# Layer 0: decayed keys and values turned by VectorE in squares of 32 and placed by DMA instead of turned by TensorE; six small operations moved from VectorE to ScalarE

## The chip, the cores and the metric

The kernel runs on one core of one Trainium2 chip. That core has a TensorE (PE in the profile, its weight loads PEld), a VectorE (DVE), a ScalarE (ACT), a GpSimd (POOL), and a SyncE (SP) whose queue issues DMAs; 16 DMA engines move the data. The metric is device microseconds of one launch, the median over runs.

## The reference

One inference step of a trunk of two layers: layer 0 mixes tokens with RWKV-7, layer 1 with differential attention. 512 prompt tokens and 32 sample tokens go through both layers; what the change touches lies in layer 0. Its token mixer, cut to what matters:

```python
def step(S, inp):
    r_t, k_t, v_t, w_t, kk_t, a_t = inp
    sa = jnp.einsum('bhvk,bhk->bhv', S, -kk_t)
    S = (S * w_t[:, :, None, :] + sa[..., None] * (kk_t * a_t)[:, :, None, :]
         + v_t[..., None] * k_t[:, :, None, :])
    return S, jnp.einsum('bhvk,bhk->bhv', S, r_t)
S_T, y = lax.scan(step, S0.astype(f32), xs)
mean = jnp.mean(y, axis=-1, keepdims=True)
var = jnp.mean(jnp.square(y - mean), axis=-1, keepdims=True)
```

There are 24 heads of 64; the state S of a head is 64x64. The projections r, k, v, the decay and the gates come from one matrix product of the normalized input with `rw_in`, in float32.

## The kernel before

Two heads are one **pair**: 128 partitions hold the two heads' 64 channels, and there are 12 pairs. The 512 prompt tokens of a pair are cut into 8 chunks of 64, and the 32 sample tokens are a ninth with a state of their own (tile SS, loaded from `state_rwkv`; PE turns it into `ps_si`). Within a chunk the recurrence is solved as a small triangular system, and only the state passes from chunk to chunk.

Per pair there is a **preparation**, `rw_prep`, a generator whose steps are set off one at a time. It makes the decay sums (`cum`, `de`), the square-root factors (`rr`, turned by PE into `ps_rt`, then `r`; used by `ps_b`), the decayed queries `zr` and decayed keys `bk` (channels on partitions, 128 columns for each chunk), the products `at` (sent by DMA to `sc1`, brought back as `m` for POOL's inversion in `rw_invert`), and at its end `bt` and `sv`: keys and values with tokens on partitions, which the recurrence uses as matmul operands. Then comes the **chain**, `rw_chain`: per chunk three matmuls into `ps_c` with copies between them, ending in the next state SB (VectorE, `chunk`). The first chunk has no state before it, and its SB is `ps_c` times the decay `dl`. After that `rw_outputs` and `rw_finish` normalize (`yt`, `gs`) and gate the result.

PE's time between these steps is filled with the main projection: `ps_g` matmuls, three for each product since float32 is carried as two parts (`hh`, `hl` for activations, `whi`, `wlo` for weights). A weight tile is loaded on SP into one of five `raw` buffers when the block two before it begins; ScalarE makes `whi` from it and VectorE `wlo`.

What sets the order: every engine, SP's queue too, works in the order in which the program issues (class `Queue`, `tie`). Pairs 0 and 1 are prepared with `FILL0` and `FILL1`, which count the `ps_g` matmuls set after each step. From then on the table `PLAN` has 23 rows for each pair's chain; a row names the steps of other pairs' work set there (`prep` 2 is the preparation of the pair two ahead) with due times, by which the `ps_g` are put between. The preparation of a pair so begins three pairs ahead and ends in the first rows of the pair before it. The last pair's last steps of preparation run at the end of pair 9, with the loads of the memory attention (`cmt`, turned by PE into `ps_ck`) right behind. One of the pairs also loads four `lam` rows for layer 1.

In `rw_prep` the end is three groups of four PE transposes, one into `ps_v` and two into `ps_bt`, each copied by ScalarE to `sv` (four copies) or `bt` (two).

Of the kernel before, what the change touches and what calls it, by code (L numbers as in the profile page):

```python
# [9 lines left out]
F32 = mybir.dt.float32  # L10
# [36 lines left out]
LATER = 0.75  # L47
FULL = ("full", 0, 0, 0)
PLAN = [
    [[("val", 0, 0.95, 0), ("prep", 2, 0.1, 0)], [("prep", 2, 0, 0.42)]],  # L50
    [[("prep", 2, 0, 1.04)], [("prep", 1, 0.53, 0)]],
    [[], [("prep", 1, 0, 0), ("prep", 2, 0.56, 1.0)]],
    [[("prep", 2, 0, 0)], [("prep", 2, 0, 1.0)]],
    [[("smp", 0, 0.11, 0.28), ("prep", 1, 0.4, 0)], [("prep", 2, 0, 0.86)]],
    [[("out", -1, 0.11, 0)], [("prep", 2, 0, 0.84)]],
    [[("prep", 2, 0, 1.1), ("smp", 0, 0.21, 0.29)], [("prep", 2, 0, 0.86)]],
    [[("prep", 2, 1.1, 1.37)], [("smp", 0, 0.21, 0)]],
# [4 lines left out]
    [[("prep", 2, 0.36, 0.43), ("at", 1, 0, 0)], [("fin", -1, 0, 0.84)]],  # L62
    [[("prep", 2, 0.36, 0.43), ("fin", -1, 0, 0)], [("prep", 3, 0, 0)]],
    [[("prep", 2, 0.25, 0)], []],
    [[("fin", -1, 0, 0.98), ("smp", 0, 0.11, 0)], [("prep", 2, 0.4, 0), ("prep", 3, 0, 0.6)]],
    [[("prep", 3, 0.53, 0), ("mrg", 1, 0, 0.86)], []],
    [[("prep", 3, 0.11, 0.17), ("mrg", 1, 0.9, 0), ("rsq", 0, 0, 1.5)], []],
    [[("prep", 3, 0.33, 0), ("fin", -1, 0, 0.88)], []],
# [25 lines left out]
CU = 8 * 65 + 33  # L94
# [14 lines left out]
class Trunk:  # L109
# [529 lines left out]
    def split_roots(self):  # L639

        rr, r = self.rr, self.r20[:, :NS]
        self.ve.tensor_copy(rr[:, :NS], r)
        self.ve.tensor_tensor(rr[:, NS : 2 * NS], r, rr[:, :NS].bitcast(F32), ALU.subtract)

    def rw_prep(self, st, rkv):

        nc, p, pr = self.nc, self.rp, st["pr"]
# [16 lines left out]
        for i in range(5):  # L664
            o, c = (32 * i, 0) if i < 4 else (0, P - TS)
# [24 lines left out]
        ch = lambda t: t[:, : 8 * 65].rearrange("p (c w) -> p c w", w=65)  # L690
# [13 lines left out]
        rr = self.rr  # L704
# [3 lines left out]
        de = p.tile([P, CW], F32, tag="de", name="de", bufs=1)  # L708
# [7 lines left out]
        self.ae.copy(r4[:], pst[:, :P])  # L716
        yield
        st["dl"] = dl = self.rb.tile([P, 9], F32, tag="dl", name="dl", bufs=4)
        self.ve.tensor_copy(dl[:, :8], ch(de[:])[:, :, 64])
        self.ve.tensor_copy(dl[:, 8:9], de[:, CU - 1 : CU])  # L720

        st["zr"] = zr = self.zr[pr % 3]
        bk = self.bk
# [12 lines left out]
        r = rkv["r"]()  # L736
# [32 lines left out]
        for q in range(2):  # L769

            yield
            ps = [self.psm.tile([P, 4, 2, 64], F32, tag="m", name="ps_at") for _ in range(2)]
            for j in range(4):
                c, i, a = 4 * q + j, j // 2, j % 2
# [35 lines left out]
        for s in range(2):  # L810
            yield
            v = rkv["v"]()
# [8 lines left out]
        ps = self.psm.tile([P, 512], F32, tag="m", name="ps_bts")  # L821
# [2 lines left out]
        bt[2] = self.rb.tile([P, 1, P], F32, tag="bts", name="bts", bufs=2)  # L824
        self.ae.copy(bt[2][:, 0, :], ps[:, :P])
        self.ae.copy(sv[2][:TS, 0, :], ps[P - TS :, P : 2 * P])
        for q in range(2):
            yield
            if q:
                ps = self.psm.tile([P, 512], F32, tag="m", name="ps_v")  # L830
                for i in range(4):
                    self.te.transpose(ps[:, i * P : i * P + P], v[:, i * P : i * P + P], self.ident[:])
                pv = ps[:].rearrange("p (j c) -> p j c", j=4)
                for u in range(2):
                    if u:
                        yield
                    sv[u] = self.rb.tile([P, 4, P], F32, tag="sv", name="sv", bufs=4)
                    self.ae.copy(sv[u][:64, 0:4:2, :], pv[:64, 2 * u : 2 * u + 2])
                    self.ae.copy(sv[u][64:, 1:4:2, :], pv[64:, 2 * u : 2 * u + 2])
                yield  # L840
            ps = self.psm.tile([P, 512], F32, tag="m", name="ps_bt")
            for j in range(4):
                c = 4 * q + j
                self.te.transpose(ps[:, j * P : j * P + P], bk[:, c * P : c * P + P], self.ident[:])
            bt[q] = self.rb.tile([P, 4, P], F32, tag="bt", name="bt", bufs=4)
            self.ae.copy(bt[q][:], ps[:].rearrange("p (j c) -> p j c", j=4))

    def rw_invert(self, st):

# [104 lines left out]
    def chunk(self, st, c, S, Snew):  # L954

        nc, H, yt = self.nc, self.H, st["yt"]
        e, zs, ro, A, cv, cb = self.place(st, c)
        i = c // 2
        yield
        ps = self.psc.tile([P, 4, P], F32, tag="c", name="ps_c")  # L960
        rhs = self.avz[:, e, i, :]
        sd = None
        if c:
            self.te.matmul(ps[:, 0, :], st["zr"][:, c * P : c * P + P], S[:], start=True, stop=True)
            self.ve.tensor_tensor(rhs[zs], ps[zs, 0, :], rhs[zs], ALU.add)
            yield

        self.te.matmul(ps[:, 1, :], A[0].rearrange("p h t -> p (h t)"), rhs, start=True, stop=True)
        for h in range(2):
            self.ae.copy(cv[zs, H[h]], ps[H[h], 1, H[h]])  # L970
        if c:
            self.ae.copy(yt[ro, i, :], ps[ro, 0, :])
            sd = self.rb2.tile([P, P], F32, tag="sd", name="sd", bufs=RB)
            self.ae.activation(sd[:], S[:], AF.Copy, scale=st["dl"][:, c : c + 1])
        yield
        self.te.matmul(ps[:, 2, :], cb, cv, start=True, stop=True)
        for hc in H:
            d = st["dl"][hc, c : c + 1]
            if c == 0:
                self.ve.tensor_scalar(Snew[hc, hc], ps[hc, 2, hc], d, None, ALU.mult)  # L980
            else:
                self.ve.scalar_tensor_tensor(Snew[hc, hc], ps[hc, 2, hc], d, sd[hc, hc], ALU.mult, ALU.add)

# [10 lines left out]
    def rw_sample(self, st):  # L994

        nc, p, pr = self.nc, self.rb2, st["pr"]
        sl = self.SS[0]
        for h in range(2):
            self.se.dma_start(sl[64 * h : 64 * h + 64, 64 * h : 64 * h + 64], self.a["state_rwkv"][0, 0, 2 * pr + h])
        yield  # L1000
        ps = self.psm.tile([P, 4, P], F32, tag="m", name="ps_si")
        self.te.transpose(ps[:, 0, :], sl[:], self.ident[:])
        S = p.tile([P, P], F32, tag="ssi", name="ssi", bufs=1)
        self.ve.tensor_copy(S[:], ps[:, 0, :])
        yield from self.chunk(st, 8, S, sl)
        yield
        self.state_out(sl, self.o[8][0, 0, 2 * pr : 2 * pr + 2])
# [84 lines left out]
    def rw_finish(self, st):  # L1092

        yield
        nc, p, pr = self.nc, self.rk0, st["pr"]
        yt, bv = st["yt"], st["bv"]
        y = yt[:].rearrange("p i (h v) -> p (i h) v", h=2)
        s = p.tile([P, 10], F32, tag="gs", name="gs", bufs=1)
        self.ve.tensor_reduce(s[:], y, AX.X, ALU.add)
        self.ve.tensor_scalar(s[:], s[:], 1.0 / 64, None, ALU.mult)  # L1100
        sh = [P, 10, 64]
        yield
        self.ve.tensor_tensor(y, y, s[:].unsqueeze(2).to_broadcast(sh), ALU.subtract)
        yield
        sq = p.tile([P, 10, 64], F32, tag="gsq", name="gsq", bufs=1)
        self.ae.activation(sq[:], y, AF.Square)
        yield
        self.ve.tensor_reduce(s[:], sq[:], AX.X, ALU.add)
        self.ve.tensor_scalar(self.q20[:, NS:], s[:], 1.0 / 64, GN_EPS, ALU.mult, ALU.add)
        yield  # L1110
        self.ve.tensor_tensor(y, y, self.r20[:, NS:].unsqueeze(2).to_broadcast(sh), ALU.mult)
        yield
        for q, c0, n in ((0, 0, TP), (1, TP, TS)):
            ps = (self.psm if q else self.psx).tile([P, 512], F32, tag="m" if q else "x", name="ps_y")
            if q == 0:
                for i in range(4):
                    self.te.transpose(ps[:, i * P : i * P + P], yt[:, i, :], self.ident[:])
            else:
                self.te.transpose(ps[:, :P], yt[:, 4, :], self.ident[:])
            self.ve.scalar_tensor_tensor(bv[:, c0 : c0 + n], ps[:, :n], self.lnw[:, pr : pr + 1], bv[:, c0 : c0 + n],  # L1120
                                         ALU.mult, ALU.add)
        yield
        sg = st["gate"]()
        self.ve.scalar_tensor_tensor(sg[:], sg[:], 0.5, bv[:], ALU.mult, ALU.mult)
        self.put(pr, sg)
# [1182 lines left out]
```

## Time and profile before

| what | number |
| --- | --- |
| median of 3 runs | 1349.31 us (1349.03 to 1351.66) |
| the profiled execution | 1349.83 us |
| its span, first to last instruction | 1348.1 us |
| mean granted clock of TensorE | 0.997 |
| DMA | 150.47 MB, 370805 packets, 163177 of them under 512 B |
| q1 (all of SP's DMAs) | 42.0% of 16 engines' span |

Layer 0 takes the first half of the span; the pairs' chains run from about 130 to 660 us, one pair every 44 us or so. In a group's row stand: line, engine, operation, output and inputs, partitions x elements, count, then busy time, mean nanoseconds of one, and the idle time in front of it with what ended it. L106 is the one line by which nearly all instructions are issued, so they are told apart by tile names. In a timeline row stand start, duration, engine, operation and tiles, and in square brackets the idle time before. SPq is SP's queue, and its rows give the time of issuing, not of moving.

### The profile page before, as it was taken

How to read it: one execution, taken by the hardware profiler on the slowest of the kernel's cores; microseconds unless marked ns; L12 is line 12 of the kernel's file. 1: busy time of each engine (PE TensorE's matmuls, PEld its weight loads, DVE VectorE, ACT ScalarE, POOL GpSimd, SP SyncE). 2: the span in 40 equal slices, each digit the busy share in tenths (PEclk: the TensorE clock that was granted, in tenths of full speed). 3: DMA queues.
4: the chain of work that ended last, by engine and by line, in shares of the span. 5: the costliest groups of instructions: out<-in, count | busy, mean ns of one | idle time of the engine just before them, and what ended most of it. 6: DMA issues, size and time to landing. Idle time of an engine off the chain costs nothing. (4 is left out here: it accounts for less than half of the span.)

```text
span 1348.1 us, 31624 instructions
## 1 busy us (share of the span) xinstructions
PE 1319.8 (98%) x11662; PEld 1264.6 (94%) x11662; DVE 956.5 (71%) x2391; ACT 813.1 (60%) x2258; POOL 368.0 (27%) x833
## 2 busy tenths in 40 slices
PE   8999999999999999999999999999999999999997
PEld 6988899999999998988999999999999999999997
DVE  5766878888887888675764578876588748887343
ACT  5766777877787777665543366754476546664222
POOL 2128668666776677600000000000000001002000
PEclk9999999999999999999999999999999999999999
DMA  7443322333233322342465466652367424762321
GB/s 225 145 138 76 82 57 68 85 87 92 59 96 87 75 78 70 100 124 83 115 188 138 130 192 149 145 141 79 98 154 160 110 83 108 164 148 89 94 86 68
DMA packets 370805, 150.47 MB, mean 112 GB/s; under 512 B 163177, under 2 KB 361202, under 8 KB 370650
## 3 DMA queue, kind: packets, MB, share of 16 engines
q1 hardware_dynamic: 370586, 148.43, 42.0%
q8 instruction: 92, 1.51, 0.5%
q14 instruction: 63, 0.52, 0.1%
q10 hardware_dynamic: 64, 0.02, 0.0%
HBM read 118.00 MB, written 30.18 MB: 110 GB/s over the span
## 5 line engine op out<-in xcount | busy, mean ns | idle before, releaser
L106 PE MATMUL ps_g<-hh,wlo 128*128 128x272 f32 x1808 | 536.1, 297 | 1.1 <-DVE wlo L106 1.0
L106 PE MATMUL ps_g<-hh,whi 128*128 128x272 f32 x1808 | 533.9, 296 | 1.0 <-DVE ats L106 0.7
L106 PE MATMUL ps_g<-hl,whi 128*128 128x272 f32 x1808 | 532.7, 295 | 1.0 <-DVE hl L106 0.7
L106 PEld LDWEIGHTS ps_g<-hh,whi 128*128 128x128 f32 x1808 | 341.1, 189 | 5.9 <-DVE ats L106 0.9
L106 PEld LDWEIGHTS ps_g<-hl,whi 128*128 128x128 f32 x1808 | 340.9, 189 | 3.9 <-DVE hl L106 1.9
L106 PEld LDWEIGHTS ps_g<-hh,wlo 128*128 128x128 f32 x1808 | 340.5, 189 | 3.0 <-DVE wlo L106 1.8
L106 DVE TENSOR_TENSOR wlo<-raw,whi 128x512 fp32r<-128x512 f32 x314 | 214.4, 693 | 106.3 <-ACT whi L106 102.0
L106 ACT CAST whi<-raw 128x512 fp32r<-128x512 f32 x314 | 188.9, 619 | 116.7 <-PE ps_g L106 64.9
L868 POOL TENSOR_TENSOR tm<-u,m 102x84 f32<-102x84 f32 (+23 forms) x341 | 138.8, 407 | 117.6 <-DMA m<-sc 71.2
L870 POOL TENSOR_TENSOR u<-u,tm 102x84 f32<-102x84 f32 (+23 forms) x341 | 158.5, 465 | 26.7
L106 PE MATMUL ps_g<-hi,wlo 128*128 128x272 f32 x512 | 147.8, 289 | 1.1 <-DVE wlo L106 1.1
L106 PE MATMUL ps_g<-hi,whi 128*128 128x272 f32 x512 | 147.7, 288 | 0.0
L106 PE MATMUL ps_g<-lo,whi 128*128 128x272 f32 x512 | 147.4, 288 | 0.0
L1339 POOL TENSOR_TENSOR lo<-og,hi 128x544 fp32r<-128x544 f32 x8 | 13.2, 1651 | 378.1 <-ACT hi L106 377.6
L106 PEld LDWEIGHTS ps_g<-hi,wlo 128*128 128x128 f32 x512 | 96.4, 188 | 1.6 <-DVE wlo L106 1.5
L106 PEld LDWEIGHTS ps_g<-hi,whi 128*128 128x128 f32 x512 | 96.6, 189 | 0.0
L106 PEld LDWEIGHTS ps_g<-lo,whi 128*128 128x128 f32 x512 | 96.4, 188 | 0.0
L106 ACT ACTIVATE pt<-ps_s,snm 128x128 f32<-128x128 f32 (+3 forms) x96 | 50.3, 527 | 57.1 <-DVE snm L106 57.1
L106 DVE SCALAR_TENSOR_TENSOR SB<-ps_c,dl,sd 64x64 f32<-64x64 f32 x168 | 47.4, 282 | 26.6 <-PE ps_c L106 20.9
L106 ACT COPY sv<-ps_c 64x64 f32<-64x64 f32 x192 | 39.6, 206 | 33.1 <-PE ps_c L106 31.2
L1803 POOL MEMSET qs<- 128x128 f32 x2 | 0.3, 206 | 188.9 <-PE ps_g L106 188.9
L106 ACT ACTIVATE sg<-ps_g 128x272 f32<-128x272 f32 x64 | 25.1, 394 | 40.2 <-PE ps_g L106 36.2
(397 smaller groups left out, 2523.1 us busy)
## 6 DMA issues: line engine op xcount, KB each, us to landing
raw<-in_rw_in_dram SPq DMA_DIRECT2D x114, 256.0 KB
raw<-in_df_in_dram SPq DMA_DIRECT2D x112, 256.0 KB
raw<-in_w_out_dram SPq DMA_DIRECT2D x64, 256.0 KB
oscr<-sg SPq DMA_DIRECT2D x16, 272.0 KB
lo<-oscr SPq DMA_DIRECT2D x16, 272.0 KB
m<-sc SPq DMA_DIRECT2D x33, 128.0 KB
raw<-in_w_mem_v_dram SPq DMA_DIRECT2D x16, 256.0 KB
out_dram<-kt SPq DMA_DIRECT2D x48, 64.0 KB
```

Source lines behind the costliest of these rows:

```text
L106: return lambda *a, **k: self.trunk.tie(self, issue(*a, **k))
L868: nc.gpsimd.tensor_tensor(tm[:, :n, :wd], u3[:, :n, kx : kx + 1].to_broadcast(sh), m3[:, kx : kx + 1, kx + 1 :].to_broadcast(sh), ALU.mult)
L870: nc.gpsimd.tensor_tensor(u3[:, :n, kx + 1 :], u3[:, :n, kx + 1 :], tm[:, :n, :wd], ALU.add)
L1339: (self.nc.gpsimd if g % 2 and self.o1 else self.ve).tensor_tensor(lo[:], t, hi[:].bitcast(F32), ALU.subtract)
L1803: nc.gpsimd.memset(t[:], 0.0)
```

## The change

The two groups `ps_bt` and the group `ps_v` of each pair go from PE, and their copies from ScalarE. In their place VectorE turns a 128x512 tile in squares of 32x32 (STREAM_TRANSPOSE); four DMAs put the squares where they belong in a scratch tensor in DRAM (`tscr`, rows of 32 floats), and one DMA (`bt`) or four (`sv`) bring the turned tile back. That is 12 placements and 6 fetches for each pair on SP. The small transposes into `ps_bts`, for the sample tokens, stay on PE.

Besides, ScalarE takes the copy into `rr`, two into `dl`, the two SB of chunk 0 and the copy `ssi`; the scaling of `gs` by 1/64 is folded into the subtraction after it. `PLAN` rows 0, 1, 2, 4 and 15 are set anew.

```diff
--- before.py
+++ after.py
@@ -47,11 +47,11 @@
 LATER = 0.75
 FULL = ("full", 0, 0, 0)
 PLAN = [
-    [[("val", 0, 0.95, 0), ("prep", 2, 0.1, 0)], [("prep", 2, 0, 0.42)]],
-    [[("prep", 2, 0, 1.04)], [("prep", 1, 0.53, 0)]],
-    [[], [("prep", 1, 0, 0), ("prep", 2, 0.56, 1.0)]],
+    [[("val", 0, 0.95, 0), ("prep", 2, 0.1, 0)], [("prep", 2, 0, 0), ("prep", 1, 0, 0.71), ("prep", 1, 0, 0.71)]],
+    [[("prep", 2, 0, 1.04)], []],
+    [[], [("prep", 2, 0.56, 1.0)]],
     [[("prep", 2, 0, 0)], [("prep", 2, 0, 1.0)]],
-    [[("smp", 0, 0.11, 0.28), ("prep", 1, 0.4, 0)], [("prep", 2, 0, 0.86)]],
+    [[("smp", 0, 0.11, 0.28), ("prep", 1, 0, 0)], [("prep", 2, 0, 0.86)]],
     [[("out", -1, 0.11, 0)], [("prep", 2, 0, 0.84)]],
     [[("prep", 2, 0, 1.1), ("smp", 0, 0.21, 0.29)], [("prep", 2, 0, 0.86)]],
     [[("prep", 2, 1.1, 1.37)], [("smp", 0, 0.21, 0)]],
@@ -62,7 +62,7 @@
     [[("prep", 2, 0.36, 0.43), ("at", 1, 0, 0)], [("fin", -1, 0, 0.84)]],
     [[("prep", 2, 0.36, 0.43), ("fin", -1, 0, 0)], [("prep", 3, 0, 0)]],
     [[("prep", 2, 0.25, 0)], []],
-    [[("fin", -1, 0, 0.98), ("smp", 0, 0.11, 0)], [("prep", 2, 0.4, 0), ("prep", 3, 0, 0.6)]],
+    [[("fin", -1, 0, 0.98), ("smp", 0, 0.11, 0)], [("prep", 2, 0, 0.71), ("prep", 3, 0, 0.6)]],
     [[("prep", 3, 0.53, 0), ("mrg", 1, 0, 0.86)], []],
     [[("prep", 3, 0.11, 0.17), ("mrg", 1, 0.9, 0), ("rsq", 0, 0, 1.5)], []],
     [[("prep", 3, 0.33, 0), ("fin", -1, 0, 0.88)], []],
@@ -639,7 +639,7 @@
     def split_roots(self):
 
         rr, r = self.rr, self.r20[:, :NS]
-        self.ve.tensor_copy(rr[:, :NS], r)
+        self.ae.copy(rr[:, :NS], r)
         self.ve.tensor_tensor(rr[:, NS : 2 * NS], r, rr[:, :NS].bitcast(F32), ALU.subtract)
 
     def rw_prep(self, st, rkv):
@@ -716,8 +716,8 @@
         self.ae.copy(r4[:], pst[:, :P])
         yield
         st["dl"] = dl = self.rb.tile([P, 9], F32, tag="dl", name="dl", bufs=4)
-        self.ve.tensor_copy(dl[:, :8], ch(de[:])[:, :, 64])
-        self.ve.tensor_copy(dl[:, 8:9], de[:, CU - 1 : CU])
+        self.ae.copy(dl[:, :8], ch(de[:])[:, :, 64])
+        self.ae.copy(dl[:, 8:9], de[:, CU - 1 : CU])
 
         st["zr"] = zr = self.zr[pr % 3]
         bk = self.bk
@@ -824,26 +824,38 @@
         bt[2] = self.rb.tile([P, 1, P], F32, tag="bts", name="bts", bufs=2)
         self.ae.copy(bt[2][:, 0, :], ps[:, :P])
         self.ae.copy(sv[2][:TS, 0, :], ps[P - TS :, P : 2 * P])
+        scr = [self.dp.tile([TP, P], F32, tag=f"tscr{n}", name=f"tscr{n}", bufs=2) for n in range(3)]
+
+        def turned(t, x, to):
+
+            t = t[:].rearrange("p j c -> p (j c)")
+            self.ve.transpose(t, x)
+            to = to[:].rearrange("(b i) (a c) -> a i b c", i=TS, c=TS)
+            for a in range(4):
+                u = slice(TS * a, TS * a + TS)
+                self.se.dma_start(to[a], t[u, :].rearrange("i (b c) -> i b c", c=TS))
+
+        def fetched(q):
+
+            self.se.dma_start(bt[q][:], scr[q][:].rearrange("(j p) c -> p j c", p=P))
+
         for q in range(2):
             yield
             if q:
-                ps = self.psm.tile([P, 512], F32, tag="m", name="ps_v")
-                for i in range(4):
-                    self.te.transpose(ps[:, i * P : i * P + P], v[:, i * P : i * P + P], self.ident[:])
-                pv = ps[:].rearrange("p (j c) -> p j c", j=4)
-                for u in range(2):
-                    if u:
-                        yield
-                    sv[u] = self.rb.tile([P, 4, P], F32, tag="sv", name="sv", bufs=4)
-                    self.ae.copy(sv[u][:64, 0:4:2, :], pv[:64, 2 * u : 2 * u + 2])
-                    self.ae.copy(sv[u][64:, 1:4:2, :], pv[64:, 2 * u : 2 * u + 2])
-                yield
-            ps = self.psm.tile([P, 512], F32, tag="m", name="ps_bt")
-            for j in range(4):
-                c = 4 * q + j
-                self.te.transpose(ps[:, j * P : j * P + P], bk[:, c * P : c * P + P], self.ident[:])
+                fetched(0)
             bt[q] = self.rb.tile([P, 4, P], F32, tag="bt", name="bt", bufs=4)
-            self.ae.copy(bt[q][:], ps[:].rearrange("p (j c) -> p j c", j=4))
+            turned(bt[q], bk[:, q * 512 : q * 512 + 512], scr[q])
+        yield
+        for u in range(2):
+            sv[u] = self.rb.tile([P, 4, P], F32, tag="sv", name="sv", bufs=4)
+        turned(sv[0], v[:, :TP], scr[2])
+        yield
+        fetched(1)
+        for u in range(2):
+            for e in range(2):
+                w = slice(64 * e, 64 * e + 64)
+                self.se.dma_start(sv[u][w, e:4:2, :],
+                                  scr[2][u * 2 * P : u * 2 * P + 2 * P].rearrange("(j p) c -> p j c", p=P)[w])
 
     def rw_invert(self, st):
 
@@ -977,7 +989,7 @@
         for hc in H:
             d = st["dl"][hc, c : c + 1]
             if c == 0:
-                self.ve.tensor_scalar(Snew[hc, hc], ps[hc, 2, hc], d, None, ALU.mult)
+                self.ae.activation(Snew[hc, hc], ps[hc, 2, hc], AF.Copy, scale=d)
             else:
                 self.ve.scalar_tensor_tensor(Snew[hc, hc], ps[hc, 2, hc], d, sd[hc, hc], ALU.mult, ALU.add)
 
@@ -1001,7 +1013,7 @@
         ps = self.psm.tile([P, 4, P], F32, tag="m", name="ps_si")
         self.te.transpose(ps[:, 0, :], sl[:], self.ident[:])
         S = p.tile([P, P], F32, tag="ssi", name="ssi", bufs=1)
-        self.ve.tensor_copy(S[:], ps[:, 0, :])
+        self.ae.copy(S[:], ps[:, 0, :])
         yield from self.chunk(st, 8, S, sl)
         yield
         self.state_out(sl, self.o[8][0, 0, 2 * pr : 2 * pr + 2])
@@ -1097,10 +1109,9 @@
         y = yt[:].rearrange("p i (h v) -> p (i h) v", h=2)
         s = p.tile([P, 10], F32, tag="gs", name="gs", bufs=1)
         self.ve.tensor_reduce(s[:], y, AX.X, ALU.add)
-        self.ve.tensor_scalar(s[:], s[:], 1.0 / 64, None, ALU.mult)
         sh = [P, 10, 64]
         yield
-        self.ve.tensor_tensor(y, y, s[:].unsqueeze(2).to_broadcast(sh), ALU.subtract)
+        self.ve.scalar_tensor_tensor(y, s[:].unsqueeze(2).to_broadcast(sh), -1.0 / 64, y, ALU.mult, ALU.add)
         yield
         sq = p.tile([P, 10, 64], F32, tag="gsq", name="gsq", bufs=1)
         self.ae.activation(sq[:], y, AF.Square)
```

Three places in the order. **First, SP's queue in a pair in the middle of layer 0**, from the gate's scratch store `oscr` to the state store `out_dram<-so`; `up` are the small low-rank weights. Before:

```order
L106 DMA oscr_475<-sg_83 128x544
L106 DMA up<-in_rw_w_up_dram 64x128 x2
L106 DMA up<-in_rw_a_up_dram 64x128 x2
L106 DMA raw<-in_rw_in_dram 128x4x128 x2
L106 DMA SS<-in_state_rwkv_dram 64x64 x2
L106 DMA out_dram<-so 128x64
```

Now:

```order
L106 DMA tscr_3119<-bt 32x16x32 x4
L106 DMA oscr_475<-sg_83 128x544
L106 DMA up<-in_rw_w_up_dram 64x128 x2
L106 DMA up<-in_rw_a_up_dram 64x128 x2
L106 DMA bt<-tscr_3119 128x4x128
L106 DMA tscr_3120<-bt 32x16x32 x4
L106 DMA tscr_3121<-sv 32x16x32 x4
L106 DMA raw<-in_rw_in_dram 128x4x128 x2
L106 DMA SS<-in_state_rwkv_dram 64x64 x2
L106 DMA bt<-tscr_3120 128x4x128
L106 DMA sv<-tscr_3121 64x2x128 x4
```

The load of `raw` and that of SS now stand behind eight placements, whose tiles VectorE turns after the last SB of the pair before.

**Second, SP's queue at the start, when pair 0's preparation ends.** `m` are the loads for POOL's inversion; `raw` the next weight tile; `memt` belongs to the prompt's memory keys. Before:

```order
L106 DMA m_1165<-sc_1146 32x1024
L106 DMA m_1165<-sc_1146 2x1024
L106 DMA raw<-in_rw_in_dram 128x4x128 x2
L106 DMA out_dram<-memt 128x2x128
L106 DMA mkv_781<-memt 128x256
```

Now:

```order
L106 DMA m_1165<-sc_1146 2x1024
L106 DMA tscr_1251<-bt 32x16x32 x4
L106 DMA bt<-tscr_1251 128x4x128
L106 DMA tscr_1252<-bt 32x16x32 x4
L106 DMA tscr_1253<-sv 32x16x32 x4
L106 DMA bt<-tscr_1252 128x4x128
L106 DMA sv<-tscr_1253 64x2x128 x4
L106 DMA raw<-in_rw_in_dram 128x4x128 x2
L106 DMA out_dram<-memt 128x2x128
```

All 18 DMAs of pair 0 stand between the loads of `m` and that weight tile. At the end of pair 9 pair 11's DMAs come to stand in the same way ahead of the load of `cmt`.

**Third, the state after chunk 0, SB, which goes from VectorE to ScalarE**, at the first chunk of a pair's chain. On VectorE before (`zr` is the next preparation's):

```order
L106 SCALAR_TENSOR_TENSOR SB_538<-ps_c,dl,sd 64x64 x2
L106 COPY dl<-de 128x8
L106 COPY dl<-de 128x1
L106 TENSOR_SCALAR SB_541<-ps_c,dl 64x64 x2
L106 TENSOR_TENSOR zr_87<-rkv,de 128x4x2x64
```

On ScalarE now (`r`, `shc`, `rkv`, `raw_486` and `dl` belong to other pairs' preparation and shift):

```order
L106 CAST r_2662<-ps_rt 128x128
L106 COPY shc<-raw_486 128x2
L106 ACTIVATE rkv<-raw_486,dv 128x544
L106 COPY raw_486<-PC 128x1
L106 COPY dl<-de 128x8
L106 COPY dl<-de 128x1
L106 ACTIVATE SB_541<-ps_c,dl 64x64 x2
L106 CAST whi<-raw 128x512 x2
```

SB of chunk 0 had only two small copies between it and the SB of the pair before; now it stands behind `r`, `rkv` and three small copies. On PE the matmul that reads it, `ps_c<-SB,zr`, stands 12 `ps_g` behind the one that it comes from; before it was 9 `ps_g` and the group `ps_v`.

## The prediction

> **What bounds the kernel now.** I read the busy times of the page first, then the page's chain of work that ended last, then busy time by stretch of layer 0.
>
> ```profile
> PE 1319.8 (98%) x11662; PEld 1264.6 (94%) x11662; DVE 956.5 (71%) x2391; ACT 813.1 (60%) x2258; POOL 368.0 (27%) x833
> PE 41%; DVE 1%; issue 0%; ACT 0%; DMA 0%; DVEq 0%; ACTq 0%
> 210.00:250.00 40.00, 40.00 (x440) 38.13 (x439) 32.76 (x82) 30.23 (x88) 27.06 (x60) 1.00 0.33 87
> 1140.00:1160.00 20.00, 20.00 (x163) 19.97 (x162) 16.56 (x45) 14.06 (x42) 0.00 (x0) 1.00 0.76 175
> ```
>
> TensorE (PE) is busy for 98% of the span, and the last chain names hardly anything else. In the stretch 210 to 250 us (columns: window, its sum, busy time of PE, PEld, DVE, ACT, POOL, granted clock, DMA share, GB/s) PE has no idle time at all, VectorE 7 of 40 us, ScalarE 10 of 40. So a PE slot that is removed is time gained, and anything else costs only where PE is made to wait. Every step below is therefore put to one question: does PE stand still? The profiled execution took 1349.83 us, 0.04% over the median of 1349.31; the sum is made against it.
>
> **What goes.** Each head pair drops three groups of four transposes on PE, and the copies that followed them.
>
> ```profile
> L106 ACT COPY sv<-ps_v 64x256 f32<-64x256 f32 x48 | 17.6, 367 | 1.3 <-PE ps_v L106 0.7
> L106 PE MATMUL ps_bt<-ident,bk 128*128 128x128 f32 x96 | 14.4, 273 | 0.0
> L106 ACT COPY bt<-ps_bt 128x512 f32<-128x512 f32 x24 | 14.1, 586 | 1.1 <-PE ps_bt L106 0.9
> L106 DVE STREAM_TRANSPOSE vb<-v 128x512 f32<-128x512 f32 x12 | 8.5, 710 | 0.0
> L106 PE MATMUL ps_v<-ident,rkv 128*128 128x128 f32 x48 | 7.2, 273 | 0.6 <-ACT svs L106 0.6
> ```
> ```profile
> 261.38 0.29 PE L106 MATMUL ps_g<-hh,whi 128*128 128x272 f32 x1
> 261.51 0.29 PE L106 MATMUL ps_g<-hl,whi 128*128 128x272 f32 x1
> 261.64 0.60 PE L106 MATMUL ps_v<-ident,rkv 128*128 128x128 f32 x4
> 262.00 0.37 PE L106 MATMUL ps_g<-hh,wlo 128*128 128x272 f32 x1
> 262.20 0.29 PE L106 MATMUL ps_g<-hh,whi 128*128 128x272 f32 x1
> ```
>
> Matmuls overlap, so the price is the distance between starts. Neighbouring ps_g start 0.13 us apart; from 261.51 to 262.20 there would be two such steps, 0.25 us, and there are 0.69, so a group costs PE 0.44 us. There are 96/4 + 48/4 = 36 groups: 36 x 0.44 = **15.8 us** of pure PE time. The one wait that these rows show, 0.6 us for svs, falls in pair 0 and goes too.
>
> ScalarE loses 2 x 0.586 + 4 x 0.367 = 2.64 us a pair. VectorE gains three transposes, priced by vb<-v of layer 1 at 0.71, 2.13 us a pair, and gives up the small operations below.
>
> ```profile
> 258.43 0.57 DVE L106 SCALAR_TENSOR_TENSOR SB<-ps_c,dl,sd 64x64 f32<-64x64 f32 x2
> 259.01 0.36 DVE L106 COPY dl<-de 128x8 f32<-128x8 f32 x2
> 261.09 0.58 DVE L106 TENSOR_SCALAR SB<-ps_c,dl 64x64 f32<-64x64 f32 x2 [1.71 <-PE ps_c L106]
> ```
>
> The dl copies (0.36) and the two SB of chunk 0 (0.58) are over half of it; with rr and ssi, which go to ScalarE too, and the scaling of gs, which is folded into the next operation, some 1.5 us leave. VectorE ends about 0.6 us a pair up and ScalarE about 1 us down; against 7 and 10 idle us in each 40 us neither becomes the bound, and I cost both at nothing where their order covers them. rr keeps its place on VectorE with one wait on ScalarE's copy, and I see no row of PE that it makes late. The SB of chunk 0 is the exception:
>
> ```profile
> 261.07 0.27 ACT L106 CAST r<-ps_rt 128x128 fp32r<-128x128 f32 x1
> 261.33 0.75 ACT L106 ACTIVATE rkv<-raw,dv 128x544 f32<-128x544 f32 x1
> 262.46 0.38 PE L106 MATMUL ps_c<-SB,zr 128*128 128x128 f32 x2
> L106 ACT COPY sv<-ps_c 64x64 f32<-64x64 f32 x192 | 39.6, 206 | 33.1 <-PE ps_c L106 31.2
> ```
>
> On ScalarE it now stands behind r, rkv, a small copy and the two dl copies. rkv ends at 262.08, three small copies at 0.2 end at 262.7, and the two SB, at the 206 ns of a 64x64 copy, at 263.1, where VectorE had them at 261.67. PE asks at 262.4 (below): a stall of **0.7 us a pair**, which the next wait of the same pair takes in. Bounds 0 and 1.4, by ScalarE's rows being that much earlier or later.
>
> Layer 1's rows were taken while POOL was idle, and in layer 0 POOL is busy for 27 of 40 us. [...]
>
> **What is added on SP.** Each pair gains 12 placement DMAs (tscr), each waiting on its transposed tile, and 6 fetches that wait for placements to land. They stand in SP's one queue, in which all that comes later waits. The nearest rows are layer 1's, which place the same kind of 32x32 squares:
>
> ```profile
> 1145.70 1.96 SPq L106 DMA_DIRECT2D ascr<-og  x4
> 1149.70 0.37 SPq L106 DMA_DIRECT2D og<-ascr  x1
> 1203.20 2.65 SPq L106 DMA_DIRECT2D vscr<-vb  x4
> 1207.90 0.38 SPq L106 DMA_DIRECT2D vt<-vscr  x1
> ```
>
> Four issues take 1.96 to 2.65 us; I take 0.49 each, the lower row, because the 2.65 spans queue waits. A fetch starts 1207.90 - 1205.85 = 2.05 us after the last placement was issued (2.04 in the other pair of rows): that is my landing time, for placements and, for want of a nearer row, for SS.
>
> **Place 1, pairs 1 to 9: SS late.** Before, SP issued the sample state SS right after raw; PE's ps_si is the first to need it.
>
> ```profile
> 258.26 1.14 SPq L106 DMA_DIRECT2D raw<-in_rw_in_dram  x2
> 259.49 1.12 SPq L106 DMA_DIRECT2D SS<-in_state_rwkv_dram  x2
> 266.44 0.27 PE L106 MATMUL ps_si<-ident,SS 128*128 128x128 f32 x1
> ```
>
> Now eight placements, those of the second bt and of sv, stand ahead of raw and SS, and their transposes stand behind the last SB on VectorE. By the rows: SB ends at 259.00, two turns end at 259.7 and 260.4, eight issues from 259.7 end at 263.6, raw at 264.85 (1.14 and a gap), SS at 265.95, SS has landed at 268.0. PE would be ready for ps_si at about 266.4: a group is gone before it, but three more ps_g are set in its place. So PE loses **1.6 us a pair** between the chunk before and ps_si, the 0.7 at SB and 0.9 more here; in nine pairs 14.4. It comes back in each pair, since the SB that starts the chain hangs on PE. Bounds: nothing, if SS lands within 0.4 us of its issue; 3.0 with issues at 2.65 for four. I take 1.6, nearest to both landing rows.
>
> In one pair four lam loads stand between raw and SS:
>
> ```profile
> 347.10 0.51 SPq L106 DMA_DIRECT2D lam<-in_df_lq_dram  x1
> 349.84 1.11 SPq L106 DMA_DIRECT2D SS<-in_state_rwkv_dram  x2
> ```
>
> They push SS by 349.84 - 347.10 = 2.7 us more: **+2.7**, bounds 0 and 2.7.
>
> **Place 2, pair 0: raw late.** Here all 18 DMAs follow the six m<-sc, ahead of the raw pair that the next whi needs.
>
> ```profile
> 84.08 2.02 SPq L106 DMA_DIRECT2D m<-sc  x6
> 86.20 1.30 SPq L106 DMA_DIRECT2D raw<-in_rw_in_dram  x2
> 94.48 0.62 ACT L106 CAST whi<-raw 128x512 fp32r<-128x512 f32 x1
> 98.80 0.27 ACT L106 CAST r<-ps_rt 128x128 fp32r<-128x128 f32 x1
> 99.11 0.73 PE L106 MATMUL ps_b<-r,hs 128*128 128x128 f32 x5 [0.72 <-ACT r L106]
> 127.59 0.98 SPq L106 DMA_DIRECT2D raw<-in_rw_in_dram  x2
> 130.62 0.62 ACT L106 CAST whi<-raw 128x512 fp32r<-128x512 f32 x1 [0.41 <-DMA raw<-in_rw_in_dram]
> ```
>
> From 86.10: four placements to 88.1, landed 90.1, fetch to 90.5, eight placements to 94.4, landed 96.5, four sv fetches at about 0.4 to 98.1. Raw goes out then, not at 86.20, and is there 130.62 - 127.59 = 3.03 later, at 101.1. ScalarE's row for that whi stands ahead of ta, de, cum and r, so r, which ScalarE reached at 98.80 after a whi at 94.48, slips by 6.6 us, and ps_b starts at 105.7 instead of 99.11: **+6.6**. The three groups of pair 0 and the svs wait are swallowed by it, so 33 groups, 14.5 us, remain as the gain. Bounds: 0 (whi has slack that I cannot see) and 9 (four issues at 2.65).
>
> **Place 3, pair 11: cmt late.** Its placements end up at the end of pair 9, ahead of the loads of layer 1's memory keys.
>
> ```profile
> 560.12 0.57 DVE L106 SCALAR_TENSOR_TENSOR SB<-ps_c,dl,sd 64x64 f32<-64x64 f32 x2
> 562.27 0.37 SPq L106 DMA_DIRECT2D cmt<-in_cache_mem_k_dram  x1
> 566.76 0.38 PE L106 MATMUL ps_ck<-ident,cmt 128*128 128x128 f32 x2
> ```
>
> SB ends at 560.7, the first turn at 561.4, eight issues at 565.3, landed 567.4, four sv fetches 569.1, cmt issued by 569.5 and landed at 571.5. PE is there at 566.76 less one group, 566.3: **+5.2**, bounds 0 and 7.
>
> **Sum.** -14.5 + 14.4 + 2.7 + 6.6 + 5.2 = +14.4: 1349.83 + 14.4 = **1364 us**. The saving is real, and SP's queue spends it twice.
>
> **The rivals.**
> A. SS is in time after all (it lands within 0.4 us, or issues take 0.2 us less): places 2 and 3 and the SB wait, -14.5 + 6.6 + 5.2 + 9 x 0.7 = +3.6, 1353.4; without the SB wait 1347.1. For it: 1.6 us is a small difference of large numbers. Against: the SP rows are in program order.
> B. Faster: nothing that SP holds back is needed in time. The full 15.8 + 0.6 come out, 1333.4. It decides at one point, whether raw of pair 0 and cmt have more than 5 to 7 us of unseen slack and SS as above. For it: PE has no idle time from 170 to 530, so no supplier is late now. Against: the three consumers stand 6 to 9 us behind their issues, and the queue shifts them by 5 to 12.
> C. Slower still: placements in 128-byte rows land slowly while weights stream, 2 us more each: 9 x 2 in the pairs, 4 at pair 0 (two landings in a row), 2 at pair 11, 24 in all: 1388. For it: a DMA share of 0.33 that the added small rows raise. Against: between 1140 and 1160 the share is 0.76 with the same kind of placements, PE has 20.00 of 20.00, and the fetch waits 2.04 us.
> [...]
>
> **How the numbers follow.** Forecast 0.60, A 0.15, B 0.14, C 0.11; the likeliest is 1364. With the bounds of the SS stall the forecast alone runs from 1350 to 1377. The range takes in A and the lower half of C: **1343 to 1382**, leaving out B and about half of C, 0.2. A run of this kernel can tell 0.2%, 2.7 us, from no change. Faster: B and a little of A, 0.17. Same: about half of A and the forecast's low end, 0.13. Slower: the rest, 0.70.
>
> **What would show it.** ps_bt and ps_v<-ident gone from PE, 144 transposes fewer. ps_si with an idle time before it, ended by the DMA SS, 1 to 2 us in nine pairs and more where lam is loaded; ps_c<-SB,zr behind ACT SB by some 0.7; the ps_b that stood at 99 waiting for r until about 106; ps_ck waiting for cmt. Idle PE in 170 to 530 us, where there is none now, of some 17 us. I am wrong if PE is still at 40.00 of 40 there, or if the wait is on bt or sv themselves, or on VectorE.

## The result, and the profile after

| | before | after |
| --- | --- | --- |
| median | 1349.6 us (4 runs) | 1414.6 us (4 runs, 1414.24 to 1420.59) |
| ratio, 95% interval | | 1.0489, 1.0459 to 1.0519 |
| span of the profiled execution | 1348.1 us | 1412.9 us |
| mean granted clock of TensorE | 0.997 | 0.983 |

The change makes the kernel 65 us slower; forecast was +14, with 1382 us as the upper end. The page of after, its busy times:

```profile
PE 1324.1 (94%) x11518; PEld 1263.8 (89%) x11518; DVE 963.4 (68%) x2343; ACT 798.0 (56%) x2258; POOL 353.2 (25%) x833
q1 hardware_dynamic: 466202, 167.32, 46.9%
```

The 144 transposes are gone (11662 - 11518), and yet PE is busy 4 us longer than before, in a span 65 us longer. PE's waits in after (what it waited for, us in total, times, longest):

```profile
PE ps_si L106 <- DMA SS<-in_state_rwkv_dram: 27.7, 11, 4.9
PE ps_b L106 <- ACT r L106: 11.4, 1, 11.4
PE ps_c L106 <- ACT SB L106: 7.0, 10, 1.4
PE ps_ck L106 <- DMA cmt<-in_cache_mem_k_dram: 6.0, 1, 6.0
PE ps_at L106 <- DVE bk L106: 5.4, 10, 1.5
...
PE ps_w L106 <- DVE bv L106: 2.9, 7, 0.4
PE ps_mkt L106 <- ACT memx L106: 2.9, 2, 1.6
```

The first four are the four waits of the prediction, in its three places. ps_at, ps_w and ps_mkt are not in it; before they waited 0.3, nothing on bv, and 0.6 us. Together these seven grew by 61.7 us (63.3 less the 0.7, 0.6 and 0.3 that were there). Against them stand 36 x 0.44 = 15.8 us less work and the svs wait of 0.6. That makes +45 us, 20 short of the 65. Most of the rest is in the clock column, here around one of the waits (window, busy times of PE, PEld, DVE, ACT and POOL, granted clock, DMA share, GB/s):

```profile
242.00:246.00 4.00, 1.31 (x11) 1.16 (x10) 1.41 (x4) 1.04 (x3) 3.29 (x10) 1.00 0.80 229
246.00:249.50 3.50, 3.50 (x18) 3.50 (x17) 1.84 (x4) 1.83 (x6) 2.87 (x9) 0.51 0.68 192
249.50:253.00 3.50, 2.73 (x24) 2.54 (x23) 2.40 (x5) 1.78 (x6) 1.99 (x4) 1.00 0.03 8
```

and on PE in the timeline, ahead of 246 and behind it (start, duration):

```profile
245.64 0.29 PE L106 MATMUL ps_g<-hh,wlo 128*128 128x272 f32 x1
245.76 0.29 PE L106 MATMUL ps_g<-hh,whi 128*128 128x272 f32 x1
...
248.44 0.43 PE L106 MATMUL ps_g<-hl,whi 128*128 128x272 f32 x1
248.66 0.43 PE L106 MATMUL ps_g<-hh,wlo 128*128 128x272 f32 x1
```

PE idles for 2.7 us of the first window, and for the next 3.4 us the granted clock is one half: ps_g start 0.22 us apart instead of 0.12. PE counts as busy there, which is why its busy time did not fall. Over the whole span the mean clock went from 0.997 to 0.983, and 0.014 x 1413 would be 20 us. But not all of this is lost, since half clock costs nothing while PE waits anyway. Layer 0 has eight half-clock stretches in after; here are the longest of them, most of which lies in ps_b's wait, and the sum of all eight:

```profile
106.09:116.33 10.24, 3.94 (x17) 3.94 (x18) 6.10 (x10) 4.79 (x12) 8.83 (x19) 0.50 0.84 241
sum 40.99, PE 31.14 PEld 30.96 DVE 14.78 ACT 15.85 POOL 30.38; mean PE 3.89 PEld 3.87 DVE 1.85 ACT 1.98 POOL 3.80
```

PE works for 31.1 us at half clock, and before for 3.4 us (at 131). At half the pace the difference costs **14 us**, an estimate. The last 6 us are, as an estimate too, the edges of the waits: a wait is counted from the end of the last matmul, 0.29 us behind its start, while in a running stream the next one starts after 0.12 us. PE waits 70 times in after and 36 times before, and 34 x 0.17 = 6 us.

How SS came to be late, in the pair at 293 us (SP's queue, VectorE, PE):

```profile
282.99 0.57 DVE L106 SCALAR_TENSOR_TENSOR SB<-ps_c,dl,sd 64x64 f32<-64x64 f32 x2
283.59 0.71 DVE L106 STREAM_TRANSPOSE bt<-bk 128x512 f32<-128x512 f32 x1
284.23 0.67 DVE L106 STREAM_TRANSPOSE sv<-rkv 128x512 f32<-128x512 f32 x1
284.33 1.95 SPq L106 DMA_DIRECT2D tscr<-bt  x4
286.38 2.10 SPq L106 DMA_DIRECT2D tscr<-sv  x4
288.52 1.07 SPq L106 DMA_DIRECT2D raw<-in_rw_in_dram  x2
289.69 1.11 SPq L106 DMA_DIRECT2D SS<-in_state_rwkv_dram  x2
287.29 0.49 PE L106 MATMUL ps_c<-SB,zr 128*128 128x128 f32 x2 [0.56 <-ACT SB L106]
293.14 0.30 PE L106 MATMUL ps_si<-ident,SS 128*128 128x128 f32 x1 [1.59 <-DMA SS<-in_state_rwkv_dram]
```

This is the chain of the prediction, row for row: SB, two turns, eight issues, raw, SS, and 2.3 us of landing (290.80 to 293.14); the pair pays 0.56 + 1.59 = 2.15 us where 1.6 were forecast. In the pair before it, raw's two issues took more:

```profile
239.18 2.29 SPq L106 DMA_DIRECT2D raw<-in_rw_in_dram  x2
241.57 1.11 SPq L106 DMA_DIRECT2D SS<-in_state_rwkv_dram  x2
244.88 0.30 PE L106 MATMUL ps_si<-ident,SS 128*128 128x128 f32 x1 [2.69 <-DMA SS<-in_state_rwkv_dram]
```

With that microsecond more the wait is 2.69 us, and 3.4 us of half clock follow it (the windows above are this pair's). Behind the 1.59 us of the pair at 293 the clock stays at 1.00 (294 to 297.5 us).

The transposes themselves, 0.71 and 0.67 us, cost no more than layer 1's 0.71, though POOL is at work beside them (1.19 of the 1.50 us from 283.5 to 285).

### The profile page after: what moved, and what is told of

It is laid out like the page before. It is cut to its first block, busy times and chain, and to the rows that moved or that the text cites. A ratio compares the mean times of both kernels' runs of the same rounds, so it can differ in the third digit from the quotient of the medians.

```text
span 1412.9 us, 31604 instructions
## 1 busy us (share of the span) xinstructions
PE 1324.1 (94%) x11518; PEld 1263.8 (89%) x11518; DVE 963.4 (68%) x2343; ACT 798.0 (56%) x2258; POOL 353.2 (25%) x833
## 5 line engine op out<-in xcount | busy, mean ns | idle before, releaser
L106 PEld LDWEIGHTS ps_g<-hh,whi 128*128 128x128 f32 x1808 | 345.6, 192 | 4.9 <-issue 0.7
L106 PEld LDWEIGHTS ps_g<-hl,whi 128*128 128x128 f32 x1808 | 344.9, 191 | 3.9 <-DVE hl L106 1.8
L106 PEld LDWEIGHTS ps_g<-hh,wlo 128*128 128x128 f32 x1808 | 344.8, 191 | 2.9 <-DVE wlo L106 1.9
L880 POOL TENSOR_TENSOR tm<-u,m 102x84 f32<-102x84 f32 (+23 forms) x341 | 144.2, 423 | 101.7 <-DMA m<-sc 73.1
L882 POOL TENSOR_TENSOR u<-u,tm 102x84 f32<-102x84 f32 (+23 forms) x341 | 138.1, 405 | 26.7
L106 DVE TENSOR_TENSOR avz<-ps_c,avz 64x128 f32<-64x128 f32 x96 | 27.5, 287 | 61.3 <-PE ps_c L106 60.1
L106 ACT COPY raw<-ps_g 128x272 f32<-128x272 f32 x74 | 28.4, 386 | 44.3 <-PE ps_g L106 43.8
```

The source lines that it names most:

```text
L106: return lambda *a, **k: self.trunk.tie(self, issue(*a, **k))
L880: nc.gpsimd.tensor_tensor(tm[:, :n, :wd], u3[:, :n, kx : kx + 1].to_broadcast(sh), m3[:, kx : kx + 1, kx + 1 :].to_broadcast(sh), ALU.mult)
L882: nc.gpsimd.tensor_tensor(u3[:, :n, kx + 1 :], u3[:, :n, kx + 1 :], tm[:, :n, :wd], ALU.add)
```

## The experiments

Two theories of the loss. **Q**: SP's queue makes SS, raw and cmt late, and PE's long waits halve its clock besides. **D**: the added traffic as such (DMA share up from 0.33 to 0.45 between 150 and 590 us) makes late whatever comes from DRAM.

**e1_ss_early.** SS of pairs 1 to 11 is asked for at row 18 of the pair before. Traffic unchanged.

```diff
                     go("chain", pr)
+                    if k == 18 and pr + 1 < NPAIR:
+                        self.sample_in(pr + 1)
```

> Theory Q (SP's queue, and the clock that drops after long waits): the state SS of pairs 1 to 11 is asked for at row 18 of the pair before, ahead of the placements; the traffic is unchanged. The waits of ps_si in pairs 1 to 9 (24.7 of the 27.7 us) go, and with them the half-clock stretches that follow them (246, 341, 392, 536 and 584 us, about 10 us lost); pair 0's wait stays. 1414.6 - 34 = 1381 us, 1374 to 1390. Theory D (the added DMA traffic itself makes whatever comes from DRAM late): another load takes the place of SS, and the time stays above 1400.

Measured 1378.8 us, ratio 1.0217 (1.0202 to 1.0231). PE's waits in it:

```profile
PE ps_b L106 <- ACT r L106: 11.5, 1, 11.5
PE ps_c L106 <- ACT SB L106: 7.0, 10, 1.4
PE ps_ck L106 <- DMA cmt<-in_cache_mem_k_dram: 6.4, 1, 6.4
PE ps_at L106 <- DVE bk L106: 4.9, 10, 0.9
...
PE ps_si L106 <- DMA SS<-in_state_rwkv_dram: 2.2, 1, 2.2
```

25.5 us of ps_si go and the time falls by 35.8: the waits cost themselves and some 10 us of clock, since PE now works for 10.1 us at half clock and not for 31.1. The DMA share between 150 and 590 us is even higher (0.49), so it was the place in the queue, not the traffic. D falls for SS. Nor does a wait here show rival C: in after the fetch of pair 0's first bt goes out 1.95 us behind the end of its placements' issues (rows under place 2 below), no later than layer 1's 2.04 and 2.05.

**e2_ends_on_pe.** Pairs 0 and 11 take the old transposes, the other ten the new path.

```diff
+        if pr in (0, NPAIR - 1):
...
+            return
         scr = [self.dp.tile([TP, P], F32, tag=f"tscr{n}", name=f"tscr{n}", bufs=2) for n in range(3)]
```

> Pairs 0 and 11 are turned on TensorE as before, the other ten by VectorE and DMA. Theory Q: the wait of ps_b for r (11.4 us) and of ps_ck for cmt (6.0) go, the half-clock stretches at 106 and 628 with them (3 to 6 us of loss), and six groups of transposes come back on PE (2.6 us): 1395 us, 1389 to 1401. Theory D: the ends are late because of traffic, which is hardly less: over 1405.

Measured 1398.5 us, 1.0361 (1.0347 to 1.0376). The waits of ps_b for r (0.8 left) and of ps_ck are gone. So places 2 and 3 are worth 16 us net. e2 takes these DMAs away together with their traffic, so it does not part Q from D for the two places; what speaks for Q there is the order of SP's rows in after, where raw goes out behind pair 0's last fetch (under place 2 below).

**e3_six_only.** The kernel before with the six small operations and the folded scaling, nothing else (the diff is those lines of the change).

> The kernel before with the six small operations (and the folded scaling) moved and nothing else; table and transposes as before. Theory Q with the SB wait: ps_c<-SB waits about 0.7 us in ten pairs for ScalarE, no half clock: 1349.6 + 7 = 1356.5 us, 1352 to 1360. Rival: ScalarE has the time, the six cost nothing: 1348 to 1351.

Measured 1358.4 us, 1.0070 (1.0058 to 1.0083).

```profile
PE ps_c L106 <- ACT SB L106: 6.0, 10, 1.5
...
PE ps_mkt L106 <- ACT memx L106: 3.5, 4, 1.6
```

The first is new and the second was 0.6 before: the operations that were to unload VectorE cost 9 us by themselves, 6.0 for SB behind ScalarE's rows, near the 7 expected, and 2.9 more at the start.

**e4_turn_only.** The opposite half: turning by VectorE and DMA, the six operations and the scaling back on VectorE.

> The change without the six small operations (they and the scaling are back on VectorE). Theory Q: the 7.0 us of waits for ACT SB go, but SS is bound to the chunk before, not to PE, so ps_si waits longer by as much; 1411 to 1417 us. Rival: the waits add up, and 7 us come out: 1405 to 1409.

Measured 1419.1 us, 1.0514 (1.0499 to 1.0529), slower than the whole change and 2 us over the band expected.

```profile
PE ps_si L106 <- DMA SS<-in_state_rwkv_dram: 36.5, 11, 5.6
PE ps_b L106 <- ACT r L106: 13.0, 1, 13.0
```

No wait for SB any more, and ps_si waits 8.8 us longer: the two do not add up, since SS is timed by the chunk before and PE merely arrives earlier. It is worse than even, and the clock shows why: PE works for 45.7 us at half clock, where it was 31.1. In place of two shorter waits in a pair (27.7 + 7.0 us in all) there was one long one of nearly the same sum (36.5).

**e5_ss_ends.** e1 and e2 together.

> SS of pairs 1 to 11 asked for early and pairs 0 and 11 turned on TensorE, both at once. Theory Q, by the waits left in the run with SS early: 1378.8 less ps_b for r (10.8 more than before), ps_ck for cmt (6.4) and the half clock beside them (8 us), plus six groups back (2.6): 1356 us, 1352 to 1363; no half-clock stretch between 150 and 700 us. Theory D: other loads become late, over 1368.

Measured 1360.2 us, 1.0084 (1.0067 to 1.0101). One half-clock stretch is left between 140 and 700 us. It stands at 147, at the very edge of the part for which none was expected, and follows pair 0's ps_si (3.0 us), whose SS stays where it was. Theory Q holds.

**e6_ss_ends_sb.** Besides, dl and the SB of chunk 0 back on VectorE, and pair 0's SS early.

```diff
-                self.ae.activation(Snew[hc, hc], ps[hc, 2, hc], AF.Copy, scale=d)
+                self.ve.tensor_scalar(Snew[hc, hc], ps[hc, 2, hc], d, None, ALU.mult)
```

> As the run before, and the SB of chunk 0 and the dl copies are back on VectorE, and pair 0's SS is asked for early too. Now nothing stands behind the SB wait to take it in, so its 7 us should come out here (where undoing all six with SS late gained nothing), and 2 us of pair 0's SS: 1347 us, 1343 to 1352. Rival: something else (ps_at for bk) takes it in again: 1353 or more.

Measured 1352.7 us, 1.0031 (1.0020 to 1.0042): 7.5 us less than e5, just above the band expected, and still not below the kernel before, though thirty groups (13 us) are gone. Its waits name what eats them (ps_mkt waited 0.6 before, ps_at 0.3, ps_w not for bv):

```profile
PE ps_at L106 <- DVE bk L106: 5.3, 10, 0.9
...
PE ps_mkt L106 <- ACT memx L106: 3.4, 3, 1.6
PE ps_w L106 <- DVE bv L106: 2.9, 7, 0.4
```

**e7_late_10 and e8_late_16.** A delay alone: the kernel before, with ten or sixteen placements that nobody reads, in front of SS in pairs 1 to 9.

```diff
+        if 0 < pr < 10:
...
+            for n in range(16):
+                a, u = n % 4, slice(TS * (n % 4), TS * (n % 4) + TS)
+                self.se.dma_start(scr[n // 4][:].rearrange("(b i) (a c) -> a i b c", i=TS, c=TS)[a],
+                                  st["bt"][1][u].rearrange("i j c -> i (j c)").rearrange("i (b c) -> i b c", c=TS))
```

> The kernel before, transposes on TensorE, with ten placements that nobody reads put ahead of SS in pairs 1 to 9 on SP (the same squares of bt, to DRAM): a delay alone. Ten issues of 0.49 us against a slack of some 3.5 us (7 where lam is loaded: 0.7, and 13 in pair 1): waits of 1.4 us in seven pairs and 4 in one, 14 us, one half-clock stretch at most: 1349 + 16 = 1365, 1357 to 1370.

> The same with sixteen placements: waits of 4.3 us in seven pairs and 7 in one, 37 us in all. If long waits also bring the clock down, 1.7 us or more is added behind each of the eight, with half-clock stretches of 3.4 us seen there: 1400 us, 1395 to 1412. If waits cost only themselves: 1386.

Measured 1378.8 us (1.0219, 1.0197 to 1.0242) and 1408.4 us (1.0447, 1.0431 to 1.0462). PE's waits, of e7 and then of e8:

```profile
PE ps_si L106 <- DMA SS<-in_state_rwkv_dram: 19.5, 8, 4.4
```
```profile
PE ps_si L106 <- DMA SS<-in_state_rwkv_dram: 43.4, 8, 7.6
```

e8 lies in its band, e7 missed its own, and the queue shows why: ten in a row take 0.70 us each on average, not 0.49, and the waits were 2.4 us each, on average too, and not the 1.4 expected in most.

```profile
263.03 7.04 SPq L106 DMA_DIRECT2D tscr<-bt  x10
270.17 1.11 SPq L106 DMA_DIRECT2D SS<-in_state_rwkv_dram  x2
```

With all transposes still on PE, waits of 19.5 us cost 30.0 (1378.8 - 1348.8) and waits of 43.4 cost 59.6: 10 and 16 us more than themselves. PE works for 22.8 us at half clock in e7 and for 32.8 in e8, against 3.4 before; half of the difference is 10 and 15 us (the mean clock alone, 0.979 in e8, would make that 25). So the clock is nearly all of it, and the working that gave 14 us for the change holds on a delay alone.

**e9_tuned_a, e10_tuned_b.** e6 with rr back on VectorE and the first bt's turn moved from row 15 to row 18, with a due time in row 0 set back; e10 also puts four more ps_g ahead of ps_at. The two rows:

```diff
-    [[("fin", -1, 0, 0.98), ("smp", 0, 0.11, 0)], [("prep", 2, 0, 0.71), ("prep", 3, 0, 0.6)]],
+    [[("fin", -1, 0, 0.98), ("smp", 0, 0.11, 0)], [("prep", 3, 0, 0.6)]],
...
-    [[("prep", 3, 0.33, 0), ("fin", -1, 0, 0.88)], []],
+    [[("prep", 3, 0.33, 0), ("fin", -1, 0, 0.88)], [("prep", 2, 0, 0.71)]],
```

> As e6, and the turn of the first bt goes from row 15 of the table to row 18 (behind the merge that ps_w waits for), and the copy into rr goes back to VectorE. Theory: in e6 PE's waits of ps_w (2.9 us) come from that turn on VectorE, and those of ps_mkt for memx (3.4, before 0.6) from rr on ScalarE at the start; both go, ps_at's 5.3 stay: 1352.7 - 5.7 = 1347 us, 1344 to 1350. Rival: VectorE's added 2.1 us a pair are late somewhere else then: 1351 or more.

> As e9, and row 6 of the table counts 0.6 us less for TensorE, which puts four more ps_g between ps_si and the ps_at that waits for bk on VectorE. Theory: the wait of ps_at goes, and the thirty groups saved come out at last: 1347 - 5 = 1342 us, 1339 to 1346, faster than both kernels. Rival: the wait moves to the next consumer of VectorE: as e9.

Measured 1366.1 us in both (1.0117, 1.0100 to 1.0134, and 1.0118, 1.0103 to 1.0133). Both expectations missed. e9's waits:

```profile
PE ps_at L106 <- DVE bk L106: 7.7, 10, 1.3
PE ps_g L106 <- DVE wlo L106: 7.0, 11, 1.0
PE ps_c L106 <- DVE SB L106: 4.2, 9, 0.6
PE ps_y L106 <- DVE yt L106: 4.1, 8, 0.9
```

ps_mkt is back at 0.6, so rr on ScalarE was its cause, and ps_w's wait for bv is gone. But every wait at the top is now for VectorE, at other places: the rival came true. In e10 ps_at falls to 2.6 us, and another wait for VectorE takes its place:

```profile
PE ps_g L106 <- DVE wlo L106: 13.5, 12, 1.6
```

Row 18 is no free place for 0.71 us of VectorE; other rows were not tried.

**e11_row6, e12_sv_pe.** e11 leaves the turn in row 15 (rr on VectorE, four more ps_g ahead of ps_at). e12 is e11 with sv turned on TensorE again in all pairs, half of the 0.6 us in row 6, and rows 0 and 1 set for it (one step of the preparation goes from row 0 to row 1). The main part of e12:

```diff
-        turned(sv[0], v[:, :TP], scr[2])
+        ps = self.psm.tile([P, 512], F32, tag="m", name="ps_v")
+        for i in range(4):
+            self.te.transpose(ps[:, i * P : i * P + P], v[:, i * P : i * P + P], self.ident[:])
...
+            self.ae.copy(sv[u][:64, 0:4:2, :], pv[:64, 2 * u : 2 * u + 2])
+            self.ae.copy(sv[u][64:, 1:4:2, :], pv[64:, 2 * u : 2 * u + 2])
```

> As e6 with the turn of the first bt left in row 15, rr back on VectorE, and row 6 counting 0.6 us less (four more ps_g ahead of ps_at). If moving the turn to row 18 was what spoiled e9 and e10: e6's 1352.7 less ps_mkt (2.8) and most of ps_at (3 to 5): 1346 us, 1343 to 1349, the first version faster than before. Rival (VectorE's load as such, wherever the turn stands): ps_g then waits for wlo or SB instead: 1350 or more.

> As e11, with sv turned on TensorE in all pairs (ps_v as before: 0.44 us a pair back on PE, 4.4 us in ten pairs; 0.71 us less on VectorE) and row 6 counting 0.3 less. If VectorE is what waits: ps_at and ps_w do not wait any more, 1349.6 - 20 x 0.44 = 1341 us, 1338 to 1346, less than e11. Rival (VectorE is not late any more in e11): slower than e11 by 4 us.

e11: 1354.6 us, 1.0037 (1.0025 to 1.0050), above its band. It differs from e10 only in the turn's row and that due time of row 0, and these are worth 11 us. ps_at is down to 0.9 us, but ps_w waits for VectorE, 7.7 us in all, and nothing is won against e6:

```profile
PE ps_w L106 <- DVE t1b L106: 3.9, 3, 3.1
PE ps_w L106 <- DVE bv L106: 3.8, 7, 0.5
```

e12: **1344.8 us, 0.9964 (0.9951 to 0.9978)**, faster than both kernels and 10 us below e11, with a third of the transposes back on PE.

```profile
PE ps_c L106 <- DVE SB L106: 5.4, 7, 1.1
...
PE ps_g L106 <- DVE wlo L106: 2.8, 5, 1.0
```

So 0.44 us more of PE in a pair, which spare VectorE 0.71, are paid back more than twice. e12 also takes eight DMAs a pair from SP and sets the rows anew; since the waits that e11 adds name VectorE and no DMA, I take VectorE for the cause, but the three were not tried apart. Twenty groups at 0.44 are 8.8 us and 5 of them arrive; SB's wait of 5.4 us (0.5 before) is the largest that is new.

## Why the prediction was wrong

The direction, the three places and the queue as the cause were right; the size was not: +14.4 forecast, +65 measured. Two things failed. Place 1 was mis-sized: 34.7 us of waits for the 17.1 in the sum. And the sum has no term for what the waits do to the clock (14 us) and none for VectorE (8 us), which was put at nothing. By its own terms:

- **What goes**: 15.8 us and 0.6. The transposes went. Right as far as it can be seen.
- **Place 1, SS and SB, +17.1** (14.4 and 2.7 for lam): PE waited 27.7 + 7.0 = 34.7 us. This is the term that is off by most. It had 0.9 us for SS behind SB, and SS took 1.5 to 3.6 us in the pairs 1 to 9, and 4.9 where lam is loaded. I had priced every issue at its lower row: the eight placements take 4.15 to 5.16 us and not 3.92, raw's two issues up to 2.29 and not 1.14, landing some 2.3 and not 2.05. That is about 1.0 of the 1.5 us a pair that are missing in these nine pairs; where the rest comes from is not shown. Pair 0's SS (2.2 us in e1, where it is the only one left) I had not counted at all. The bound of 3.0 us a pair did not hold either: SB and SS together pass it in five of the eight pairs without lam, at 585 us with 5.0.
- **The SB wait, 0.7 a pair, taken in by the next**: right, 7.0 us in ten pairs, and e4 shows that it is taken in.
- **Place 2, +6.6**: ps_b came at 112.39 instead of 99.11. The steps were as told, but started later, and the issues were slower:

```profile
89.89 3.63 SPq L106 DMA_DIRECT2D tscr<-bt  x4
95.47 0.38 SPq L106 DMA_DIRECT2D bt<-tscr  x1
...
104.52 1.14 SPq L106 DMA_DIRECT2D raw<-in_rw_in_dram  x2
107.74 0.62 ACT L106 CAST whi<-raw 128x512 fp32r<-128x512 f32 x1 [10.57 <-DMA raw<-in_rw_in_dram]
112.39 1.25 PE L106 MATMUL ps_b<-r,hs 128*128 128x128 f32 x5 [11.42 <-ACT r L106]
```

  Raw went out at 104.5, not 98.1. Of these 6.4 us the start is 3.8 (the m loads are out at 89.8, not 86.1), the first four placements are 1.6, and the sv fetches 1.0. As a wait it is 11.4 us, where the working comes to 9.2 (105.7 less the 96.5 at which PE would have stood without the old wait of 0.7 and the 1.9 us of pair 0's groups and svs).
- **Place 3, +5.2**: 6.0 us. Right.
- **"I cost both at nothing"** (VectorE and ScalarE): wrong. The reading that failed is that 7 idle us in each 40 cover 0.6 us more. ps_at and ps_w wait 8 us for VectorE in after, which the prediction itself had named as a sign of being wrong; e9 to e11 push this wait about without losing it, and e12, which gives VectorE 0.71 us back, is the first to gain. Nor was rr on ScalarE free: ps_mkt waits 2.3 us longer at the start (2.9 in e3; none in e9, with rr on VectorE).
- **What the sum left out altogether**: a wait is priced at its length, everywhere in it. The clock took 14 us more, which e7 and e8 show on a delay alone, and the edges of the waits some 6, an estimate. The prediction's first fence already had the column in which the clock shows.

The differences add up: place 1 17.6 (34.7 - 17.1), clock 14, VectorE 8, edges 6, places 2 and 3 some 3, ps_mkt 2.3: 51 us, against 50.6 between the forecast's +14.4 and +65.0. Two of these terms are estimates, so that the sum closes to 1 us is in part luck. Rivals A and B did not happen, nor C: its number, 1388, was nearer, but where a fetch shows it (pair 0), placements landed no later than in layer 1 (1.95 us against 2.04 and 2.05), no run shows the 2 us more for each landing that its number is made of, and e1 got the waits back with the same traffic. One reading in the case against B was off: ps_ck stood 4.5 us behind the issue of cmt, not 6 to 9, which speaks against B all the more.

## What to carry to other kernels

Before moving work to a queue that is in order, list what is issued behind it and when that is needed; in e1 one load, issued earlier, gave back 36 of 65 us. Where an engine is at 100%, look at the supplier's free time in the rows where the new work would stand, not at its share. And a stall of TensorE was not always priced by its length here: in e3, at a mean clock of 0.997 as before, 9 us of short waits cost 9 us; in after, eight of the twelve stalls of 1.5 us or more had 3.4 to 10.2 us of half clock in or behind them, which cost as well as far as TensorE had work in it.

## What the runs showed of the hardware

In before and after the granted clock is 1.00 or 0.50 and nothing between. The ends aside, half clock came in after in eight stretches, five of 3.41 us, two of 6.83 and one of 10.24, and in before in one of 3.41 (at 131). PE's waits of 1.5 us or more in after, from 60 us on:

| PE waits from (us) | for (us) | half clock in or behind it |
| --- | --- | --- |
| 62.2 | 1.58 | 3.41 us from 65.1 |
| 101.0 | 11.42 | 10.24 us from 106.1 |
| 153.0 | 2.67 | none |
| 242.2 | 2.69 | 3.41 us from 246.0 |
| 291.5 | 1.59 | none |
| 337.9 | 3.00 | 3.41 us from 341.6 |
| 388.1 | 4.92 | 3.41 us from 392.8 |
| 439.2 | 2.76 | none |
| 486.7 | 2.87 | none |
| 534.0 | 1.89 | 3.41 us from 536.2 |
| 581.4 | 3.60 | 6.83 us from 584.0 |
| 624.7 | 5.95 | 6.83 us from 628.3 |

Length alone does not part them: 2.87 us passed, and 1.58 and 1.89 did not. The stretches between two changes of the clock, at half and at full, are whole multiples of 3.41 us in both profiles (1 to 354 of them, the ends aside). Counted in such steps, up to 1400 us of after, PE had 1.81 us of idle time or more in the eight steps at full clock that were followed by half, and 1.78 or less in all others at full clock; of the twelve at half clock, the four with 0.98 us or more were followed by another, the eight with 0.22 or less were not. In before the one step that was followed by half, at 128 us, had 0.45 us of idle time; what halved the clock there is not shown.

The issue of a DMA on SP had no fixed price here: the same two loads of raw took 1.07 and 2.29 us in neighbouring pairs of after, and the placements 0.49 us each in one row of four (at 284 us in after), 0.91 in another (at 90 us), and 0.70 in e7's row of ten.
